# Attention heads in pairs on opposite partition halves, in a two-block transformer kernel on one core

## The chip, the core and the metric

The kernel runs on one core of a Trainium2 chip. The metric is the time on the device in microseconds; 2528.64 us is the median of three runs before (2525.15 to 2530.93). The core has a matrix engine (TensorE, PE in the profile, with its weight loads as PEld), VectorE (DVE), ScalarE (ACT), GpSimd (POOL), a queue engine (SyncE, SP) that issues the transfers, and 16 DMA engines. Matrix products write to PSUM, which DVE and ACT read.

## What is computed

Two transformer blocks on 256 tokens of width 2048, in float32. The change lies in the first block's mixer, which has four kinds of heads. Cut to what matters:

```python
def fox_attention(q, k, v, f_logit, f_bias):      # 7 heads of 64: "forgetting"
    cum = jnp.cumsum(log_sigmoid(f_logit + f_bias), axis=1)
    s = einsum(q, k) * scale + cum_q - cum_k       # causal
    return einsum(softmax(s), v)

def nsa_attention(...):                            # 8 heads of 64, 2 groups of keys
    o_c = einsum(softmax(q @ kc + bias), vc)       # 15 compressed keys
    o_s = einsum(softmax(q @ k_slc + bias), v_slc) # selected blocks
    o_w = einsum(softmax(q @ k_win + bias), v_win) # window
    return g0 * o_c + g1 * o_s + g2 * o_w

def dilated_attention(q, k, v):                    # 9 heads of 64: 3 dilations x 3
    # per dilation a softmax over its own keys; then a softmax over the three
    # log-sums of heads i, 3 + i, 6 + i weighs their outputs
    ...

def diff_attention(q, k, v, lam_vecs, ...):        # 4 heads, two maps of 64 each
    return rms_norm(einsum(softmax(s0) - lam * softmax(s1), v))

o = concat([o_fox, o_nsa, o_dil, o_diff]) @ w_out
```

At 256 tokens all selected blocks and the whole window are kept, so every map is a causal 256 x 256 table with a bias (for the dilated heads with holes). The rest of the network (modulation vectors from `ada_w`, a gated feed-forward layer, a second block with banded, recurrent and memory attention) is the same before and after.

## The kernel before

Every dense product streams its weights from memory in pieces of 128 x 1024 (`piece`, lines 284 to 295): SP loads a piece, ACT rounds it to a high part `Wh` (line 292), DVE takes the rest `Wl` (line 293), and PE multiplies both with activations that are split in the same way (`unit_b`, `unit_a`). Three buffers each hold `W`, `Wh` and `Wl`. After each piece the build calls `trickle`, which may emit one piece of background work, the scaling of a 128 x 1024 block of `ada_w` on DVE (line 431, tile `b`; 192 of them in the kernel), and `step`, which advances the attention heads. `RATES` says how many background pieces go with each weight piece in the five parts of the mixer; `settle` makes sure that enough of them are done before their results are used. So the number of weight pieces and of background pieces is fixed, whatever the heads do.

A head is a Python generator: each `yield` hands the turn back until the next weight piece. `later(n, fn)` starts one n pieces from now; `AT` holds the spacing (forgetting heads 4 pieces apart, selected-block heads 5, dilated triples 4, differential heads 4). The tile framework then orders the instructions of each engine by their order in the program and by its own estimate of when they can run. Loads through `load` (line 195: tables, background pieces) are pinned to program order on SP.

All the heads go through the same helpers:

- `scores` (line 572) makes one map: the upper 128 queries against 256 keys and the lower 128 against 128 keys, two PE products of 64 rows, for forgetting heads each followed by a product of 7 rows that adds the running sums (`sel7`, `ncum`). Each float32 product is two instructions in the trace. DVE adds a table and takes the maximum (line 589), ACT takes the exponential (line 593).
- `weigh` (line 599) scales the map, `pt` transposes it (line 192 on PE, copied by ACT in line 608), `pv` multiplies with the values, 128 rows and 64 columns for these heads: again two products.
- `put` (line 620) splits a head's 64 rows into half of one of the 16 tiles `O`, by line 626 (ACT) and line 627 (DVE).

`fox_head`, `nsa_head` and `dil_triple` handle one forgetting head, one selected-block head (a selected and a window map, then their value products and that of the compressed keys in one sum) and three dilated heads in a row. The queries and keys of head h lie on partitions 0 to 63 or 64 to 127 (`half`), alternating with h for forgetting and dilated heads; for the selected-block heads by group, heads 0 to 3 low and 4 to 7 high. Each score map takes one of four side banks of PSUM (`ps`), and so does each transposed map and each value product; the dense products have four other banks (`pd`). Everything of a head is emitted on its own, so on PE consecutive small products mostly read the same half. `diff_head` is the exception: its two maps, in the low and in the high half, are emitted one behind the other. In the second block, `rw_scan` already alternates its recurrent products between the halves.

`SLOTS`, `BUFS` and `WB` set the buffers: 14 of the 256-column temporaries `q`, 8 maps `e`, 3 transposed maps `pt`, 3 tables `tab`.

Of the kernel before, what the change touches and what calls it, by code (L numbers as in the profile page):

```python
# [111 lines left out]
AT = {"fox": 4, "nsa": 5, "dil": 4, "diff": 4, "pre": 4, "solve": 20, "a": 5, "c": 2}  # L112
# [16 lines left out]
NARROW = {"start"}  # L129

# [16 lines left out]
class Build:  # L147
# [424 lines left out]
    def scores(self, q, k, tab, fox=None):  # L572


        nc = self.nc
        p = self.ps()
        last = fox is None
        self.mm(p[:, 0:256], q[:, 128:256], k, True, last)
        if not last:
            self.mm(p[:, 0:256], fox[0], fox[1], False, True)  # L580
        self.mm(p[:, 256:384], q[:, 0:128], k[:, 0:128], True, last)
        if not last:
            self.mm(p[:, 256:384], fox[0], fox[1][:, 0:128], False, True)
        e = self.tmp((128, 384), tag="e")
        m = self.tiny(2)
        nm = self.tiny(2)
        sm = self.tiny(2)
        for a, (lo, hi, t0) in enumerate(((0, 256, 0), (256, 384, 128))):
            nc.vector.tensor_tensor_reduce(e[:, lo:hi], p[:, lo:hi], tab[:, t0:256], scale=1.0, scalar=-3e38,
                                           op0=OP.add, op1=OP.max, accum_out=m[:, a:a + 1])  # L590
        nc.vector.tensor_scalar(nm, m, -1.0, None, op0=OP.mult)  # L591
        for a, (lo, hi) in enumerate(((0, 256), (256, 384))):
            nc.scalar.activation(e[:, lo:hi], e[:, lo:hi], AF.Exp, bias=nm[:, a:a + 1],  # L593
                                 accum_out=sm[:, a:a + 1])
        return e, m, sm
# [24 lines left out]
    def put(self, n, ps):  # L620

        t, h = n // 2, (n % 2) * 64
        if self.O[t] is None:
            self.O[t] = self.slot(dt=F32R)
        o = self.O[t][h:h + 64]
        self.nc.scalar.copy(o[:, :256], ps)
        self.nc.vector.tensor_tensor(o[:, 256:], ps, o[:, :256], op=OP.subtract)
# [6 lines left out]
    def fox_head(self, h):  # L634
        q, k = self.hq[h], self.hk[h]
        tab = self.table(0)
        yield from self.wait(lambda: self.ncum is not None)
        e, m, sm = self.scores(q, k, tab, (self.sel7[h], self.ncum))
        self.weigh(e, self.recip(sm))
        yield  # L640
        t = self.pt(e)
        yield
        hf = (h % 2) * 64
        p = self.ps()[hf:hf + 64, :256]
        self.pv(p, self.fv[0][:, 64 * h:64 * h + 64], self.fv[1][:, 64 * h:64 * h + 64], t)
        self.put(h, p)

    def fox_cum(self):
# [28 lines left out]
        yield  # L677
        p = self.ps()
        self.mm(p[:7, 0:128], a[:, 0:7], self.C["trif"])
        self.mm(p[:7, 128:256], a[:, 0:7], self.ones, True, False)  # L680
        self.mm(p[:7, 128:256], a[:, 7:14], self.C["trif"], False, True)
        t = self.slot()
        v.tensor_copy(t[:7, :256], p[:7, :256])
        self.ncum = t[:7, :256]
# [100 lines left out]
    def nsa_head(self, h):  # L785
        nc = self.nc
        g = h // 4
        hf = 64 * g
        q = self.nq[h % 4][hf:hf + 64]
        n = 7 + h  # L790
        tab = self.table(1 + h)
        es = []
        yield
        for br, k in ((1, self.nks), (2, self.nkw)):
            e, m, sm = self.scores(q, k[hf:hf + 64], tab)
            f = self.recip(sm)
            for a in range(2):
                nc.vector.tensor_tensor(f[:, a:a + 1], f[:, a:a + 1], self.gate[:, 1 - a, h, br:br + 1], op=OP.mult)  # L798
            self.weigh(e, f)
            es.append(e)  # L800
            yield
        ts = [self.pt(e) for e in es]
        yield from self.wait(lambda: self.pct is not None)
        yield
        of = (n % 2) * 64
        p = self.ps()[of:of + 64, :256]
        self.mm(p, self.vcb[:, h, :], self.pct, True, False)
        for b in range(2):
            c = b * 128 + g * 64
            self.pv(p, self.nv[0][:, c:c + 64], self.nv[1][:, c:c + 64], ts[b], False, b == 1)  # L810
        self.put(n, p)

    def dil_triple(self, i):
        nc, v = self.nc, self.nc.vector
        M = self.tiny(6)
        Z = self.tiny(6)
        es = []
        for g in range(3):
            h = 3 * g + i
            tab = self.table(9 + h)  # L820
            yield
            e, m, sm = self.scores(self.dq[h], self.dk[h], tab)
            v.tensor_copy(M[:, 2 * g:2 * g + 2], m)
            v.tensor_copy(Z[:, 2 * g:2 * g + 2], sm)
            es.append(e)
        mx = self.tiny(2)
        v.tensor_tensor(mx, M[:, 0:2], M[:, 2:4], op=OP.max)
        v.tensor_tensor(mx, mx, M[:, 4:6], op=OP.max)
        M3 = M.rearrange("p (g a) -> p g a", g=3)
        v.tensor_tensor(M3, M3, mx[:, None, :].to_broadcast([128, 3, 2]), op=OP.subtract)  # L830
        nc.scalar.activation(M, M, AF.Exp)
        v.tensor_tensor(Z, Z, M, op=OP.mult)
        z = self.tiny(2)
        v.tensor_tensor(z, Z[:, 0:2], Z[:, 2:4], op=OP.add)
        v.tensor_tensor(z, z, Z[:, 4:6], op=OP.add)
        r = self.recip(z)
        v.tensor_tensor(M3, M3, r[:, None, :].to_broadcast([128, 3, 2]), op=OP.mult)
        for g in range(3):
            self.weigh(es[g], M[:, 2 * g:2 * g + 2])
        yield  # L840
        for g in range(3):
            h = 3 * g + i
            n = 15 + h
            t = self.pt(es[g])
            yield
            of = (n % 2) * 64
            p = self.ps()[of:of + 64, :256]
            vv = self.dv[0 if h < 5 else 1]
            c = 64 * (h if h < 5 else h - 5)
            self.pv(p, vv[0][:, c:c + 64], vv[1][:, c:c + 64], t)  # L850
            self.put(n, p)
# [16 lines left out]
    def diff_head(self, h):  # L868
# [4 lines left out]
        for m in range(2):  # L873
            e, _, sm = self.scores(self.fq[h][64 * m:64 * m + 64], self.fk[h][64 * m:64 * m + 64], tab)
            es.append(e)
            fs.append(self.recip(sm))
# [9 lines left out]
        self.pv(p, self.fvv[0][:, 128 * h:128 * h + 128], self.fvv[1][:, 128 * h:128 * h + 128], t)  # L886
# [16 lines left out]
    def mixer(self):  # L903
        self.narrow = "mixer" in NARROW
        I, X = self.I, self.X
        w = "w_in"
        self.consts(1)
        sel = [self.slot(), self.slot()]
        self.load(sel[0][:7, :512], I["const2"][:7, :512])
        self.load(sel[1][:7, :384], I["const2"][:7, 512:])  # L910
# [884 lines left out]
```

## Time and profile before

| | |
|---|---|
| timed runs | 2530.93, 2525.15, 2528.64 us (median 2528.64) |
| the profiled execution | 2534.44 us, its span 2532.7 us |
| TensorE busy, its weight loads | 2440.0 us (96%), 2094.4 us (83%) |
| VectorE busy | 1792.8 us (71%) |
| ScalarE busy | 1292.7 us (51%) |
| DMA, mean over the span | 208 GB/s |

"Busy" counts a product until its modelled end, so two products that follow each other closely overlap in it; what a product takes of the engine is better read from the start of one to the start of the next. The timeline merges like instructions that follow each other into one row: start, length, and how many. A chain of waits is followed back from the last instruction of a stretch: each step is the work that released the next.

### The profile page before, as it was taken

Reading aid. Unit: us, or ns where it says so; the run is one execution under the profiler, and the core shown is the slowest. Engines: PE = TensorE matmul, PEld = TensorE weight load, DVE = VectorE, ACT = ScalarE, POOL = GpSimd, SP = SyncE. Lnnn points to the kernel's source line nnn. Section 1 sums busy time; section 2 is a strip of 40 time slices with the busy share of each in tenths; the row PEclk is TensorE's granted clock in tenths of the full one; section 3 lists DMA queues with packets and bytes.
Section 4 is the critical chain, followed back from the end, with each engine's and each line's share of the span. In section 5 each row is a group of like instructions: output and inputs, shape, how many; then the busy total and the mean of one; then the engine's idle time right before and its main releaser. Section 6 shows DMA issues by size and latency. Waiting matters only on the chain.

```text
span 2532.7 us, 39262 instructions
## 1 busy us (share of the span) xinstructions
PE 2440.0 (96%) x14852; PEld 2094.4 (83%) x14852; DVE 1792.8 (71%) x3379; ACT 1292.7 (51%) x2177; POOL 55.6 (2%) x102
## 2 busy tenths in 40 slices
PE   6889999998799999999999999999999999999999
PEld 5778788776588888888888887888888888888888
DVE  8987767789767765555566788768976766666664
ACT  5345445665544444444455554566554654444443
POOL 0000000000000000000000001000020000000000
PEclk8999999999899999999999999999999999999999
DMA  8998777667578775666656655434453466666675
GB/s 323 342 338 290 223 254 262 213 231 260 191 236 273 265 240 184 193 189 190 187 185 187 210 167 177 144 117 144 157 173 121 136 191 190 190 186 191 189 228 166
DMA packets 161501, 527.51 MB, mean 208 GB/s; under 512 B 22912, under 2 KB 33303, under 8 KB 161184
## 3 DMA queue, kind: packets, MB, share of 16 engines
q1 hardware_dynamic: 157296, 516.35, 62.8%
q0 software_dynamic: 4016, 8.66, 1.0%
q8 instruction: 116, 1.90, 0.3%
q14 instruction: 73, 0.60, 0.1%
HBM read 516.54 MB, written 9.45 MB: 208 GB/s over the span
## 4 chain that ended last, share of the span: by engine, by line
PE 75%; DVE 11%; DMA 8%; issue 3%; ACT 2%; SPq 0%; ACTq 0%; DVEq 0%
PE pd L188 67%; PE ps L188 8%; DVE Wl L293 4%; DMA b<-in_ada_w_dram 4%; DVE b L431 2%; DMA W<-in_w_in_dram 2%; DMA W<-in_w_mem_kv_dram 1%; ACT Wh L292 1%; DMA W<-in_w_out_dram 1%; PE ps L192 1%; DVE dt L223 0%; DVE q L202 0%; DVE q L201 0%; DVE s L208 0%; DVE b L1247 0%
## 5 line engine op out<-in xcount | busy, mean ns | idle before, releaser
L188 PE MATMUL pd<-s,Wh 128*128 128x512 f32 (+1 forms) x5824 | 1447.8, 390 | 40.0 <-ACT Wh L292 20.2
L293 DVE TENSOR_TENSOR Wl<-W,Wh 128x1024 fp32r<-128x1024 f32 x770 | 928.2, 1208 | 536.9 <-ACT Wh L292 517.4
L292 ACT CAST Wh<-W 128x1024 fp32r<-128x1024 f32 x770 | 796.7, 1036 | 961.8 <-PE pd L188 596.9
L188 PEld LDWEIGHTS pd<-s,Wh 128*128 128x128 f32 x5824 | 1030.2, 191 | 228.0 <-ACT Wh L292 25.7
L188 PEld LDWEIGHTS pd<-s,Wl 128*128 128x128 f32 x5584 | 765.5, 191 | 66.7 <-DVE Wl L293 12.8
L188 PE MATMUL pd<-s,Wl 128*128 128x256 f32 x5584 | 791.9, 284 | 8.0 <-DVE Wl L293 7.8
L431 DVE SCALAR_TENSOR_TENSOR b<-b,tq 128x1024 f32<-128x1024 f32 x192 | 233.0, 1220 | 53.3 <-DMA b<-in_ada_w_dram 53.0
L188 PE MATMUL pd<-Wh,s 128*128 128x512 f32 (+4 forms) x576 | 164.4, 363 | 3.6 <-ACT Wh L292 3.5
L188 PEld LDWEIGHTS pd<-Wh,s 128*128 128x128 f32 x576 | 103.9, 190 | 20.9 <-ACT Wh L292 5.9
L223 DVE TENSOR_TENSOR dt<-pd,dt 128x256 f32<-128x256 f32 x289 | 110.6, 418 | 12.1 <-ACT dt L222 11.8
L188 PE MATMUL pd<-Wl,s 128*128 128x512 f32 (+4 forms) x288 | 105.5, 366 | 6.8 <-DVE Wl L293 6.8
L222 ACT COPY dt<-pd 128x256 f32<-128x256 f32 x289 | 94.7, 370 | 21.8 <-PE pd L188 19.9
L188 PE MATMUL ps<-s 64*128 64x256 f32 (+7 forms) x356 | 84.8, 369 | 5.2 <-DVE s L1553 3.0
L188 PEld LDWEIGHTS ps<-s 64*128 64x128 f32 (+4 forms) x356 | 55.0, 187 | 28.1 <-issue 11.6
L188 PEld LDWEIGHTS pd<-Wl,s 128*128 128x128 f32 x288 | 54.6, 189 | 18.2 <-DVE Wl L293 11.1
L593 ACT ACTIVATE e<-e,y 128x256 f32<-128x256 f32 x80 | 35.7, 448 | 27.5 <-DVE y L591 27.4
L188 PE MATMUL ps<-q,con 128*128 128x256 f32 x132 | 39.4, 404 | 10.7 <-ACT q L1032 3.0
L208 DVE TENSOR_TENSOR s<-q,s 128x256 fp32r<-128x256 f32 x104 | 39.8, 422 | 5.8 <-ACT s L207 5.5
L207 ACT CAST s<-q 128x256 fp32r<-128x256 f32 x104 | 37.8, 404 | 9.4 <-DVE q L1083 5.1
L188 PEld LDWEIGHTS ps<-q,con 128*128 128x128 f32 x132 | 22.7, 193 | 19.8 <-ACT q L519 4.5
L188 PE MATMUL ps<-pt,s 128*64 128x128 f32 (+3 forms) x176 | 37.4, 341 | 1.7 <-ACT pt L608 1.7
L599 ACT ACTIVATE e<-e,y 128x256 f32<-128x256 f32 x88 | 34.9, 449 | 7.5 <-DVE y L798 3.8
(292 smaller groups left out, 1339.3 us busy)
## 6 DMA issues: line engine op xcount, KB each, us to landing
W<-in_w_in_dram SPq DMA_DIRECT2D x334, 512.0 KB, 3.8
b<-in_ada_w_dram SPq DMA_DIRECT2D x192, 512.0 KB, 5.4
W<-in_ffn_w_gate_dram SPq DMA_DIRECT2D x88, 512.0 KB, 3.7
W<-in_ffn_w_up_dram SPq DMA_DIRECT2D x88, 512.0 KB, 4.0
W<-in_ffn_w_down_dram SPq DMA_DIRECT2D x80, 512.0 KB, 3.6
W<-in_w_mem_kv_dram SPq DMA_DIRECT2D x32, 512.0 KB, 6.6
W<-in_w_out_dram SPq DMA_DIRECT2D x32, 512.0 KB, 4.6
W<-in_w_o_dram SPq DMA_DIRECT2D x32, 512.0 KB, 3.9
```

Of the source, the lines that this page charges most:

```text
L188: self.nc.tensor.matmul(out, lhsT, rhs, start=start, stop=stop)
L192: self.nc.tensor.transpose(out, in_, self.ident[p0:p0 + n, p0:p0 + n])
L207: self.nc.scalar.copy(out[:, :256], src)
L208: self.nc.vector.tensor_tensor(out[:, 256:], src, out[:, :256], op=OP.subtract)
L222: self.nc.scalar.copy(t, ps[:, 256:512])
L223: self.nc.vector.tensor_tensor(t, ps[:, :256], t, op=OP.add)
L292: nc.scalar.copy(Wh[:, :n], W[:, :n])
L293: nc.vector.tensor_tensor(Wl[:, :n], W[:, :n], Wh[:, :n], op=OP.subtract)
L431: nc.vector.scalar_tensor_tensor(W, W, 1.0, self.crow[half], op0=OP.mult, op1=OP.mult, accum_out=acc[:, k:k + 1])
L593: nc.scalar.activation(e[:, lo:hi], e[:, lo:hi], AF.Exp, bias=nm[:, a:a + 1], accum_out=sm[:, a:a + 1])
L599: self.nc.scalar.activation(e[:, lo:hi], e[:, lo:hi], AF.Copy, scale=f[:, a:a + 1])
```

## The change

Two heads of opposite halves are handled together, and their products are emitted in turn, one of each head. `scores` takes a list of heads and gives each its own PSUM bank; `pv` takes a list too and writes the two heads into the two halves of one bank. Forgetting heads go in the pairs (0, 1), (2, 3), (4, 5) and head 6 alone, 8 pieces apart; selected-block heads j and j + 4, 10 apart; the dilated heads run as two tasks, the triples 0 and 1 together as the pairs (0, 3), (1, 4), (6, 7), and triple 2 as (2, 5) and 8 alone. The running sums and the selector rows stand in both halves (partitions 0 to 6 and 64 to 70). `put` writes a whole tile for a pair, which moves heads to other places in `O`; the rows of `w_out` are permuted on the way to device memory to match (`HEADS`, `ROWS`). `q` goes from 14 to 12 buffers, `pt` from 3 to 4. The calls of `pv` and `scores` in `diff_head` and `a_head` take the new form and emit what they emitted before, but for the order: the differential head's two maps now alternate.

```diff
-BUFS = {"q": 14, "dt": 6, "e": 8, "pt": 3, "tab": 3, "b2": 3, "tq": 1}
+BUFS = {"q": 12, "dt": 6, "e": 8, "pt": 4, "tab": 3, "b2": 3, "tq": 1}
-AT = {"fox": 4, "nsa": 5, "dil": 4, "diff": 4, ...}
+AT = {"fox": 8, "nsa": 10, "dil": 8, "diff": 4, ...}
+HEADS = (0, 1, 2, 3, 4, 5, 7, 11, 8, 12, 9, 13, 10, 14, 15, 18, 16, 19, 17, 20, 21, 22, 6, 23)
+ROWS = {"w_out": np.concatenate([np.arange(64 * h, 64 * h + 64) for h in HEADS] + [np.arange(1536, 2048)])}

-    def scores(self, q, k, tab, fox=None):
...
+    def scores(self, heads):
+        ps = [self.ps() for _ in heads]
+        for lo, hi, q0 in ((0, 256, 128), (256, 384, 0)):
+            n = hi - lo
+            for p, (q, k, _, fox) in zip(ps, heads):
+                self.mm(p[:, lo:hi], q[:, q0:q0 + 128], k[:, 0:n], True, fox is None)
+            for p, (_, _, _, fox) in zip(ps, heads):
+                if fox is not None:
+                    self.mm(p[:, lo:hi], fox[0], fox[1][:, 0:n], False, True)
+        out = []
+        for p, (_, _, tab, _) in zip(ps, heads):
+            e = self.tmp((128, 384), tag="e")
...
+            out.append((e, m, sm))
+        return out

-    def pv(self, o, v0, v1, t, start=True, stop=True):
-        self.mm(o, v0, t[:, 0:256], start, False)
-        self.mm(o[:, 128:256], v1, t[:, 256:384], False, stop)
+    def pv(self, heads, start=True, stop=True):
+        for o, v0, v1, t in heads:
+            self.mm(o, v0, t[:, 0:256], start, False)
+        for o, v0, v1, t in heads:
+            self.mm(o[:, 128:256], v1, t[:, 256:384], False, stop)
+
+    def halves(self, p, heads):
+        return [p[64 * a:64 * a + 64, :256] for a in range(len(heads))]

-    def put(self, n, ps):
-        t, h = n // 2, (n % 2) * 64
+    def put(self, t, ps, rows=slice(0, 128)):
...
+        o = self.O[t][rows]
+        self.nc.scalar.copy(o[:, :256], ps[rows, :256])
+        self.nc.vector.tensor_tensor(o[:, 256:], ps[rows, :256], o[:, :256], op=OP.subtract)

+    def fox_heads(self, hs):
+        tab = self.table(0)
+        yield from self.wait(lambda: self.ncum is not None)
+        es = []
+        for e, m, sm in self.scores([(self.hq[h], self.hk[h], tab, (self.sel7[h], self.ncum[h % 2])) for h in hs]):
+            self.weigh(e, self.recip(sm))
+            es.append(e)
+        yield
+        ts = [self.pt(e) for e in es]
+        yield
+        p = self.ps()
+        self.pv([(o, fv(0, h), fv(1, h), t) for o, h, t in zip(self.halves(p, hs), hs, ts)])
...
     def fox_cum(self):
...
+        both = [slice(0, 7), slice(64, 71)]
+        for s in both:
+            self.mm(p[s, 0:128], a[:, 0:7], self.C["trif"])
+            self.mm(p[s, 128:256], a[:, 0:7], self.ones, True, False)
+            self.mm(p[s, 128:256], a[:, 7:14], self.C["trif"], False, True)
+        for s in both:
+            v.tensor_copy(t[s, :256], p[s, :256])

+    def nsa_heads(self, j):
+        hs = (j, j + 4)
+        tabs = [self.table(1 + h) for h in hs]
...
+        for br, k in ((1, self.nks), (2, self.nkw)):
+            maps = self.scores([(self.nq[j][s], k[s], tab, None) for s, tab in zip(rows, tabs)])
...
+            yield
+        ts = [[self.pt(e) for e in pair] for pair in es]
...
+        for o, h in zip(os, hs):
+            self.mm(o, self.vcb[:, h, :], self.pct, True, False)
+        for b in range(2):
+            self.pv([(os[g], vv(0, g), vv(1, g), ts[b][g]) for g in range(2)], False, b == 1)
+        self.put(3 + j, p)

+    def dil_triples(self, run, pairs):
...
+        for hs, _ in pairs:
+            tabs = [self.table(9 + h) for h in hs]
+            yield
+            maps = self.scores([(self.dq[h], self.dk[h], tab, None) for h, tab in zip(hs, tabs)])
...
+        yield
+        for hs, tile in pairs:
+            ts = [self.pt(es[h]) for h in hs]
+            yield
+            p = self.ps()
+            if len(hs) == 2:
+                self.pv([(o, vv(0, h), vv(1, h), t) for o, h, t in zip(self.halves(p, hs), hs, ts)])
+                self.put(tile, p)
...
     def mixer(self):
...
+        for a in (0, 64):
+            self.load(sel[0][a:a + 7, :512], I["const2"][:7, :512])
+            self.load(sel[1][a:a + 7, :384], I["const2"][:7, 512:])
```

## Rows read from the trace of the kernel before

**Rows 1.** The page, part 1: busy us (share of the span), instructions.

```profile
PE 2440.0 (96%) x14852; PEld 2094.4 (83%) x14852; DVE 1792.8 (71%) x3379; ACT 1292.7 (51%) x2177; POOL 55.6 (2%) x102
```

**Rows 2.** Busy time by stretch: engines in us, then clock, DMA share, GB/s.

```profile
263.00:385.00 122.00, 121.64 (x711) 98.13 (x710) 86.92 (x223) 58.41 (x133) 0.00 (x0) 0.96 0.70 237
385.00:545.00 160.00, 157.23 (x877) 126.81 (x875) 115.70 (x341) 95.74 (x235) 0.00 (x0) 1.00 0.69 235
545.00:681.00 136.00, 107.25 (x540) 86.44 (x539) 123.24 (x271) 80.76 (x162) 0.00 (x0) 0.90 0.71 232
1400.00:2000.00 600.00, 589.60 (x4367) 500.91 (x4366) 465.21 (x1028) 331.71 (x562) 44.72 (x78) 1.00 0.49 154
```

**Rows 3.** The chain of waits from 263 to 385 us: shares by line.

```profile
by line: PE pd L188 64.4%; PE ps L188 29.2%; PE ps L192 3.7%; DVE b L431 0.9%; DVE Wl L293 0.9%; DVE q L742 0.2%; issue 0.1%; DVE y L727 0.1%; DVE q L740 0.1%; DVE y L435 0.1%; DVE y L729 0.1%; DVE y L730 0.1%; DVE mod L419 0.1%; DVE y L738
```

**Rows 4.** The chain of waits from 385 to 545 us: shares by line.

```profile
by line: PE pd L188 33.3%; PE ps L188 18.5%; DMA b<-in_ada_w_dram 12.6%; issue 5.2%; DVE b L431 4.8%; PE ps L192 4.7%; DVE Wl L293 4.2%; DMA W<-in_w_in_dram 3.2%; ACT e L593 2.8%; ACT e L599 1.8%; ACT Wh L292 1.3%; SPq L195 1.2%; DVE e L589
```

**Rows 5.** PE around one forgetting head in time: start us, duration us, instructions.

```profile
305.08 0.29 PE L188 MATMUL pd<-Wl,s 128*128 128x280 f32 x1
305.21 0.29 PE L188 MATMUL pd<-Wh,s 128*128 128x280 f32 x1
305.43 2.15 PE L188 MATMUL ps<-s 64*128 64x256 f32 x8
307.51 0.73 PE L188 MATMUL pd<-s,Wh 128*128 128x512 f32 x2
```

**Rows 6.** PE, value product of one forgetting head.

```profile
302.12 0.86 PE L188 MATMUL ps<-pt,s 128*64 128x256 f32 x4
302.91 0.40 PE L188 MATMUL pd<-Wh,s 128*128 128x280 f32 x1
```

**Rows 7.** PE, scores of one selected-block map.

```profile
373.64 0.92 PE L188 MATMUL ps<-s 64*128 64x256 f32 x4
374.49 0.73 PE L188 MATMUL pd<-s,Wh 128*128 128x512 f32 x2
```

**Rows 8.** PE, value products of one selected-block head.

```profile
384.61 0.65 PE L188 MATMUL ps<-s 128*64 128x256 f32 x2
...
386.49 0.41 PE L188 MATMUL pd<-Wh,s 128*128 128x320 f32 x1
```

**Rows 9.** PE, two dilated maps side by side, first place.

```profile
487.74 0.93 PE L188 MATMUL ps<-s 64*128 64x256 f32 x8
488.60 0.86 PE L188 MATMUL ps<-pt,s 128*64 128x256 f32 x4
```

**Rows 10.** PE, two dilated maps side by side, second place.

```profile
491.09 1.57 PE L188 MATMUL ps<-s 64*128 64x256 f32 x8
492.59 0.65 PE L188 MATMUL ps<-pt,s 128*64 128x256 f32 x2
```

**Rows 11.** PE, the two maps of one differential head.

```profile
547.29 0.93 PE L188 MATMUL ps<-s 64*128 64x256 f32 x8
548.15 0.74 PE L188 MATMUL pd<-s,Wl 128*128 128x256 f32 x4
```

**Rows 12.** PE, recurrent products with alternating output halves.

```profile
1665.47 0.69 PE L188 MATMUL ps<-e,s 128*64 128x64 f32 x16
1665.99 0.64 PE L188 MATMUL ps<-s,e 128*64 128x64 f32 x16
```

**Rows 13.** Both instructions of put: duration ns min/median/max, first and last start.

```profile
L626 ACT CAST s<-ps x24: 350/366/370, 271.6 to 529.9; 64x256 fp32r<-64x256 f32 x24
...
L627 DVE TENSOR_TENSOR s<-ps,s x24: 407/422/429, 272.0 to 531.5; 64x256 fp32r<-64x256 f32 x24
```

**Rows 14.** DVE, 262 to 545 us, the score reduces: busy, mean ns | idle.

```profile
L589 DVE CUSTOM_DVE_ANT_0 e<-ps,tab 128x256 f32<-128x256 f32 x68 | 22.0, 351 | 15.3 <-PE ps L188 15.1
```

**Rows 15.** PE groups by shape: the forgetting heads' running sums.

```profile
L188 PE MATMUL ps<-s,y 128*7 128x128 f32 x4 | 0.8, 274 | 0.0
```

**Rows 16.** DMA issues: the mask tables; KB each, median us to landing.

```profile
tab<-in_tabs_dram SPq DMA_DIRECT2D x28, 128.0 KB, 3.7
```

More of the change, by code (lines that the diff above doesn't have):

```diff
@@ L794, in nsa_head @@
         for br, k in ((1, self.nks), (2, self.nkw)):
[L795 to L800, printed above, removed]
+            maps = self.scores([(self.nq[j][s], k[s], tab, None) for s, tab in zip(rows, tabs)])
+            for h, (e, m, sm) in zip(hs, maps):
+                f = self.recip(sm)
+                for a in range(2):
+                    nc.vector.tensor_tensor(f[:, a:a + 1], f[:, a:a + 1], self.gate[:, 1 - a, h, br:br + 1], op=OP.mult)
+                self.weigh(e, f)
@@ L808, in nsa_head @@
         for b in range(2):
[L809 to L813, printed above, removed]
+            vv = lambda t, g: self.nv[t][:, b * 128 + g * 64:b * 128 + g * 64 + 64]
+            self.pv([(os[g], vv(0, g), vv(1, g), ts[b][g]) for g in range(2)], False, b == 1)
+        self.put(3 + j, p)
+    def dil_triples(self, run, pairs):
         nc, v = self.nc, self.nc.vector
[L815 to L820, printed above, removed]
-            yield
[L822 to L839, printed above, removed]
@@ new lines, in dil_triples @@
+        M = {i: self.tiny(6) for i in run}
+        Z = {i: self.tiny(6) for i in run}
+        es = {}
+        for hs, _ in pairs:
+            tabs = [self.table(9 + h) for h in hs]
+            yield
+            maps = self.scores([(self.dq[h], self.dk[h], tab, None) for h, tab in zip(hs, tabs)])
+            for h, (e, m, sm) in zip(hs, maps):
+                g, i = divmod(h, 3)
+                v.tensor_copy(M[i][:, 2 * g:2 * g + 2], m)
+                v.tensor_copy(Z[i][:, 2 * g:2 * g + 2], sm)
+                es[h] = e
@@ L872, in diff_head @@
         yield
-        for m in range(2):
-            e, _, sm = self.scores(self.fq[h][64 * m:64 * m + 64], self.fk[h][64 * m:64 * m + 64], tab)
+        rows = (slice(0, 64), slice(64, 128))
+        for e, _, sm in self.scores([(self.fq[h][s], self.fk[h][s], tab, None) for s in rows]):
             es.append(e)
@@ L954, in mixer @@
         self.begin(self.fox_cum)
-        for h in range(7):
-            self.later(AT["fox"] * h, lambda h=h: self.fox_head(h))
+        for i, hs in enumerate(((0, 1), (2, 3), (4, 5), (6,))):
+            self.later(AT["fox"] * i, lambda hs=hs: self.fox_heads(hs))
         self.rate = RATES[1]
@@ L970, in mixer @@
         self.begin(self.nsa_compress)
-        for h in range(8):
-            self.later(8 + AT["nsa"] * h, lambda h=h: self.nsa_head(h))
+        for j in range(4):
+            self.later(8 + AT["nsa"] * j, lambda j=j: self.nsa_heads(j))
         self.rate = RATES[2]
@@ L983, in mixer @@
         self.unit_a(X, w, [(DIL_V + 320, 256)], 256, keep(self.dv[1], 256))
-        for i in range(3):
-            self.later(4 + AT["dil"] * i, lambda i=i: self.dil_triple(i))
+        for i, (run, pairs) in enumerate((((0, 1), (((0, 3), 7), ((1, 4), 8), ((6, 7), 10))),
+                                          ((2,), (((2, 5), 9), ((8,), 11))))):
+            self.later(4 + AT["dil"] * i, lambda run=run, pairs=pairs: self.dil_triples(run, pairs))
         self.rate = RATES[3]
@@ L1757, in lay_features, with lay_blocks @@
     return x[0].T.reshape(8, 2, 128, 256).transpose(0, 2, 1, 3).reshape(8, 128, 512)
-def lay_blocks(w, specs):
+def lay_blocks(w, specs, rows=None):
     w = w.reshape(-1, w.shape[-1])
+    if rows is not None:
+        w = w[rows]
     out = []
```

112 lines of the change are left out of this document (47 added, 65 removed).

## The prediction

> **What bounds the kernel now.** The order of reading was: the shares of the engines, the same by stretch of time, the chain of waits in the stretches that the change touches, and then TensorE's own order in time around single heads. The shares say that TensorE is busy 96% of the span, DVE 71%, ACT 51% [rows 1]. By stretch that is not one kernel but three [rows 2]. From 263 to 385 us (forgetting heads, the compressed keys, the first selected-block heads) PE works 121.64 of 122 us. From 385 to 545 us (the other selected-block heads, the dilated heads) it works 157.23 of 160 us, but DVE 115.70 and the DMA engines 69% beside it. From 545 to 681 us (differential heads, output projection, the rest of the background scaling of ada_w) DVE works 123.24 of 136 us and PE only 107.25: there the supply of weights is the bound, with a fixed number of pieces. The chain tells the same more sharply. Before 385 us, 64.4 + 29.2 + 3.7 = 97% of it is PE [rows 3]: a microsecond taken off PE is a microsecond. From 385 to 545 us PE has 33.3 + 18.5 + 4.7 = 56.5%; the rest are ada_w transfers, DVE splitting weights, and issue [rows 4]: PE just keeps up with its weights, and both are late in turns.
>
> **What a small burst costs today.** The change alters the order of small PE products, so the unit is a burst of them between dense products, from its first start to the next dense start. Forgetting head: eight instructions, 305.43 to 307.51 = 2.08 us; and the dense product ahead of it held the slot 0.22 us (305.21 to 305.43) where its like took 0.13 (305.08 to 305.21), so 0.09 us to get in: 2.17 us [rows 5]. I take the same 0.09 for each burst. Its value product: 302.12 to 302.91, 0.79 + 0.09 = 0.88 us [rows 6]. One selected-block map: 0.85 + 0.09 = 0.94 us [rows 7]. The value products of such a head (compressed, selected and window part, ten instructions): 1.88 + 0.09 = 1.97 us [rows 8].
>
> **What a pair will cost.** The trace has the operation already, by chance. A differential head's two maps read partitions 0 to 63 and 64 to 127, and the eight instructions of both take 547.29 to 548.15 = 0.86 us [rows 11], against 0.85 us for the four of one map. Two dilated maps side by side take 0.86 us in one place [rows 9] and 1.50 in another [rows 10]; heads alternate between the halves, and the two places are what opposite and equal halves would give. So a pair in opposite halves costs one burst. For the value products (128 rows, 64 columns, outputs in the two halves of one bank) the nearest rows are the recurrent products: 16 instructions of 64 columns with alternating output halves, 1665.47 to 1665.99 = 0.52 us, 0.065 us for two [rows 12]; the 256-column instructions of a single head run one after the other [rows 6]. I take a pair as one burst here too. Bounds: one burst (this row) and two bursts (no overlap for long moving operands).
>
> Of that the Trainium skill speaks against the value products: "TensorE: Matmul & The Clock Gate", Part 3, The mechanism, says that a weight load overlaps running products only when the row group differs, and both halves of a value pair use all rows. In the recurrent row 0.065 us for two leaves no room for two weight loads one after the other, so this trace contradicts it at 64 columns; by that rule the pairs would gain little.
>
> **The sum on PE.** Forgetting scores: 7 bursts become 4 (three pairs and head 6): 3 x 2.17 = 6.5 us. Their value products: 3 x 0.88 = 2.6. Selected-block scores: 16 become 8: 8 x 0.94 = 7.5. Value products: 8 become 4: 4 x 1.97 = 7.9. Dilated scores: 9 maps become four pairs and one single, 5 x 0.94 = 4.70; today five single ones (the kind of rows 7), the overlapped two (0.95) and the serial two (1.59) make 7.24: 2.5. Dilated value products: 9 become 5: 4 x 0.88 = 3.5. Differential: overlapped today in three of the four heads [rows 11], 0. Together 30.5 us. Against it: the running sums are made twice, six more products at 0.2 us at most (0.8 us for four [rows 15]), I take 0.7 in all. And bursts that already stand next to another pay no 0.09: about ten, 1.0 us. Net 28.8 us of PE time: 11.8 before 385 us (all of the forgetting heads, 4 of 16 maps and 2 of 8 value products of the selected-block heads, less 0.7 and half of the 1.0), 17.0 after it.
>
> **The other edits.** `put` runs 13 times instead of 24, at the same length: 11 x 0.366 = 4.0 us less on ACT and 11 x 0.422 = 4.6 us less on DVE [rows 13]; neither ends before 385 us, after it this is a small part of the relief there. Reduces, exponentials and weighings keep their number (68 reduces [rows 14]) but come two heads at a time; before 385 us DVE's 86.92 and ACT's 58.41 of 122 us hide that, and if that cover went, the price is the second head's two reduces, 2 x 0.351 us a pair. Tables: four loads for the forgetting heads instead of seven, but now two in a step with three buffers. In the dilated run the second table of pairs two and three waits for a reduce of the pair before, on SP, with weight loads queued behind it: 0 to 2 x 3.7 us [rows 16]; I take 0, since SP runs pieces ahead, and leave it to the share below. Two more loads of the selector rows stand ahead of the first dense stretch, covered by PE work: 0. The permuted rows of w_out change where data lies, not how much. The temporaries `q` fall from 14 to 12, `pt` rises from 3 to 4: of 1400 to 2000 us PE is idle 10.4 [rows 2], mostly in the recurrent heads, which use `q` most. Bounds -1 (a transposed map that comes free earlier) to +10 (that idle time twice over); I take 0, as 98% busy PE is the nearest row.
>
> **What arrives at the end.** Before 385 us PE is the chain: 11.8 count in full. After it bounds are 0 (supply alone sets the pace) and 17.0; I take PE's share of the chain, 56.5%: 9.6. What follows from 545 us on has a fixed number of pieces and starts earlier by the same. 11.8 + 9.6 = 21.4 us. The profiled execution took 2534.44 us (span 2532.7 and 1.7 around it): 2513.0. The median of the timed runs, 2528.64, is 5.8 below it; the same gain gives 2507.2, and I forecast 2507.
>
> **Rivals.**
> Supply takes the second stretch: once PE is quicker, the ada_w transfers and DVE set the pace from 385 us on. For it: 43% of that chain, and 545 to 681 us, where the same supply is the bound at 232 GB/s, no more than the 235 here [rows 2]. Against it: DVE there has 91% to do, here 72%. Only 11.8 us arrive: 2516.8.
> The value pairs don't overlap: 2.6 + 7.9 + 3.5 = 14.0 of the 28.8 go, and the gain shrinks to 21.4 x 14.8 / 28.8 = 11.0: 2517.6. Against it rows 12. The rule of the Trainium skill named above would do the same.
> The `q` buffers cost their 10 us: 2507 + 10 = 2517.
> Slower: PSUM. The side work has four banks; a pair takes two for its scores, four transposes take four. PE runs in order, so a product that waits for a bank holds the dense ones behind it, until DVE has done the four reduces of a pair, 4 x 0.351 = 1.4 us [rows 14]. 17 score steps and 13 groups of transposes at 1.4 us are 42.0 us, less 28.8: +13.2, 2542. It decides from these 30 waits costing 0.96 us each. For it: reduces already wait for PE, not PE for them, 15.3 us [rows 14], so today no bank is short; that speaks against it.
> It doesn't do what it says: pairs run serially and nothing moves, 2528.6. Rows 11 all but exclude it.
>
> **How the numbers follow.** Forecast 60%, in its own range 2499 (all 28.8) to 2514; supply 22%; value pairs 3%; `q` 5%; PSUM 8%; no overlap 2%. A change under 0.2%, 5.1 us, can't be told from none. The forecast, 18 of the 22, 3 and 4 of the 5 are faster: 85%. The rest of those (5) and the last (2) fall within it: 7%; PSUM 8% slower. The range 2497 to 2522 holds the forecast nearly whole and the supply, value and `q` cases as far as they are faster, about 82%.
>
> **What would show it.** In the changed kernel: a selected-block score burst of eight instructions in 0.86 us, a forgetting pair of sixteen in 2.1, a value pair of eight in 0.79, twenty in 1.9. The last two-map burst of the differential heads comes about 21 us earlier. PE's share of the chain after 385 us falls and the share of ada_w transfers and DVE rises; if it rises to 545-us levels, the supply rival was right. The stretch of the recurrent heads keeps its length, or `q` was the cost. PE waiting for a reduce ahead of scores or transposes would be the PSUM case. The prediction is wrong if bursts halve and the end doesn't move, or if they don't halve.

## The result, and the profile after

The changed kernel took 2491.65 us (median of four runs, 2488.18 to 2494.37) beside 2526.91 us for the kernel before on the same chip: ratio 0.9858, 95% interval 0.9838 to 0.9877, 35 us less. On a second chip it took 2493.57 beside 2522.89 us, ratio 0.9887, interval 0.9871 to 0.9903, 29 us less. The forecast was 2507, a gain of 21.4, in a range that ended at 2497: right sign, gain too small by 8 to 14 us. Below, one of the six executions of `e_dil` took 6040.12 us; its median counts it, its ratio does not.

The profiled execution of before (2534.44 us) was longer than any of its timed runs, that of after (2488.18) was the shortest of its first four. So 46 us lie between these two traces, but not all are the change's. Two further traces help: a second one of after (2495.55 us), and one of the kernel before with only the new buffer numbers (`e_bufs` below, 2519.39 us), which differs from after in the pairs and what goes with them (the whole-tile `put`, the second copy of the running sums, the order of the rows of `w_out`).

The page's first part, which answers to [rows 1]:

```profile
PE 2404.4 (97%) x14858; PEld 2074.2 (83%) x14858; DVE 1787.0 (72%) x3369; ACT 1287.9 (52%) x2166; POOL 55.7 (2%) x102
```

PE gave up 35.6 us of busy time, DVE 5.8. The steps on PE look as foretold. Timeline of PE in after: start us, length us, instructions.

```profile
295.51 2.17 PE L193 MATMUL ps<-s 64*128 64x256 f32 x16
297.62 1.67 PE L193 MATMUL pd<-s,Wh 128*128 128x512 f32 x6
...
374.54 0.92 PE L193 MATMUL ps<-s 64*128 64x256 f32 x8
375.39 0.42 PE L193 MATMUL pd<-Wh,s 128*128 128x320 f32 x1
...
389.34 0.65 PE L193 MATMUL ps<-s 128*64 128x256 f32 x4
389.82 1.55 PE L193 MATMUL ps<-pt,s 128*64 128x256 f32 x16
391.30 0.39 PE L193 MATMUL pd<-Wl,s 128*128 128x256 f32 x1
...
446.06 0.87 PE L193 MATMUL ps<-pt,s 128*64 128x256 f32 x8
446.87 0.87 PE L197 MATMUL ps<-con,e 128*128 128x128 f32 x6
```

From start to start: a forgetting pair 2.11 us (single head 2.08, [rows 5]), a selected-block pair 0.85 (single map 0.85, [rows 7]), twenty instructions of value products 1.96 (ten in 1.88, [rows 8]), a value pair 0.81 (single 0.79, [rows 6]). Every pair costs what one head cost, value pairs too; the rule of the Trainium skill that the prediction quoted against them ("TensorE: Matmul & The Clock Gate", Part 3, The mechanism) does not hold here.

Where the time went is best seen by stretches cut at the same work. I cut at the 1200th, 1680th, 2240th and 2640th dense product: forgetting and first selected-block heads; other selected-block and dilated heads; differential heads and output projection. Busy time by stretch of before, then of `e_bufs`, after, and the second trace of after (columns as in [rows 2], the second number is the length):

```profile
260.80:388.60 127.80, 127.44 (x745) 102.68 (x744) 91.65 (x232) 60.01 (x135) 0.00 (x0) 0.96 0.70 236
388.60:537.30 148.70, 146.01 (x814) 117.80 (x813) 104.97 (x314) 88.65 (x217) 0.00 (x0) 1.00 0.68 229
537.30:637.80 100.50, 89.20 (x463) 71.85 (x461) 93.72 (x214) 62.60 (x126) 0.00 (x0) 0.95 0.80 266
```

```profile
257.00:384.60 127.60, 127.25 (x746) 103.06 (x745) 91.94 (x233) 60.12 (x135) 0.00 (x0) 0.96 0.71 240
384.60:531.40 146.80, 145.54 (x813) 117.75 (x813) 105.04 (x315) 88.97 (x217) 0.00 (x0) 1.00 0.68 231
531.40:629.60 98.20, 87.43 (x463) 70.50 (x461) 93.50 (x213) 62.80 (x126) 0.00 (x0) 0.97 0.78 273
```

```profile
253.00:371.00 118.00, 114.07 (x752) 94.59 (x752) 92.19 (x237) 58.64 (x131) 0.00 (x0) 0.99 0.79 265
371.00:501.00 130.00, 128.83 (x810) 107.55 (x809) 104.26 (x310) 85.93 (x211) 0.00 (x0) 1.00 0.80 272
501.00:596.00 95.00, 87.05 (x466) 71.18 (x465) 90.38 (x210) 62.11 (x126) 0.00 (x0) 0.96 0.79 261
```

```profile
256.00:377.00 121.00, 116.57 (x747) 96.21 (x747) 91.72 (x235) 58.94 (x131) 0.00 (x0) 0.96 0.77 256
377.00:510.00 133.00, 129.26 (x814) 108.02 (x813) 104.98 (x311) 86.28 (x211) 0.00 (x0) 1.00 0.78 267
510.00:605.00 95.00, 86.80 (x467) 71.29 (x465) 90.69 (x209) 62.38 (x126) 0.00 (x0) 0.96 0.79 261
```

Taken exactly from start to start of those products, and with the rest of the span (us):

| | until the first cut | first stretch | second | third | after it |
|---|---|---|---|---|---|
| before | 260.8 | 127.9 | 148.6 | 100.5 | 1894.9 |
| `e_bufs` | 257.0 | 127.6 | 146.8 | 98.2 | 1888.0 |
| after, two traces | 253.3, 255.8 | 117.9, 121.6 | 130.3, 132.8 | 94.7, 94.4 | 1890.0, 1889.0 |
| after less `e_bufs` | -3.7, -1.2 | -9.7, -6.0 | -16.5, -14.0 | -3.5, -3.8 | +2.0, +1.0 |
| forecast | 0 | -11.8 | -9.6 | 0 | 0 |

After the last cut before took 5 to 7 us more than the three other traces, `e_bufs` included: scatter of that execution. Against `e_bufs` the pairs are worth 24 to 31 us; the buffers add some 2 by the ratio of the timed runs, 5 at most by its interval. Before the first cut executions scatter as much as the table shows: `x_before` below, the same program as `e_bufs` up to there, took 260.6 us. In the first stretch the two traces of after differ by 3.7 us, and most of that is TensorE's clock (0.99 and 0.96). Length times granted clock, an estimate of the length at full clock where PE is nearly always busy, is 122.7 and 122.5 us in before and `e_bufs`, 116.8 and 116.2 in the two of after: some 6 us for the pairs. In the second stretch the clock was 1.00 throughout.

The chain of waits by line in after, first stretch (253 to 371 us), then second (371 to 501 us):

```profile
by line: PE pd L193 48.4%; PE ps L193 17.2%; DVE b L436 6.2%; DVE Wl L298 5.2%; DMA b<-in_ada_w_dram 4.7%; DMA W<-in_w_in_dram 3.7%; PE ps L197 3.0%; issue 2.8%; ACT Wh L297 2.6%; DVE e L598 2.1%; ACT e L609 1.9%; ACT e L602 1.7%; ACT s L97
...
by line: PE pd L193 58.1%; PE ps L193 8.7%; PE ps L197 5.4%; issue 3.6%; DVE Wl L298 3.6%; DMA b<-in_ada_w_dram 3.5%; DMA tab<-in_tabs_dram 3.1%; DVE b L436 3.0%; DVE e L598 2.4%; ACT e L602 2.1%; ACT Wh L297 1.6%; ACT e L609 1.2%; DVE s L6
```

PE's share fell from 97% [rows 3] to 68.6% in the first, and rose from 56.5% [rows 4] to 72.2% in the second, where the prediction looked for a fall. The recurrent heads, which use `q` most, did not change: 589.83 us of PE in 600 (1350 to 1950 us), as before [rows 2].

### The profile page after: what moved, and what is told of

The parts are those of the page before. It is cut to its first block, busy times and chain, and to the rows that moved or that the text cites. A ratio compares the mean times of both kernels' runs of the same rounds, so it can differ in the third digit from the quotient of the medians.

```text
span 2486.3 us, 39252 instructions
## 1 busy us (share of the span) xinstructions
PE 2404.4 (97%) x14858; PEld 2074.2 (83%) x14858; DVE 1787.0 (72%) x3369; ACT 1287.9 (52%) x2166; POOL 55.7 (2%) x102
## 4 chain that ended last, share of the span: by engine, by line
PE 78%; DVE 12%; DMA 5%; ACT 2%; issue 2%; POOL 0%; SPq 0%; DVEq 0%; ACTq 0%
PE pd L193 70%; PE ps L193 7%; DVE Wl L298 4%; DVE b L436 2%; DMA W<-in_w_in_dram 2%; DMA b<-in_ada_w_dram 1%; DMA W<-in_w_mem_kv_dram 1%; ACT Wh L297 1%; PE ps L197 1%; DMA W<-in_w_out_dram 1%; DVE e L598 0%; DVE dt L228 0%; DVE b L1279 0%; DVE q L207 0%; DVE q L206 0%
## 5 line engine op out<-in xcount | busy, mean ns | idle before, releaser
L436 DVE SCALAR_TENSOR_TENSOR b<-b,tq 128x1024 f32<-128x1024 f32 x192 | 232.8, 1218 | 10.3 <-DMA b<-in_ada_w_dram 9.9
L193 PE MATMUL ps<-s 64*128 64x256 f32 (+7 forms) x356 | 65.8, 366 | 4.5 <-DVE s L1585 3.6
L193 PEld LDWEIGHTS ps<-s 64*128 64x128 f32 (+4 forms) x356 | 44.0, 186 | 21.2 <-issue 6.1
L193 PE MATMUL ps<-q,con 128*128 128x256 f32 x132 | 38.8, 400 | 12.9 <-ACT q L1064 3.7
```

The costliest lines, as they stand in the source:

```text
L193: self.nc.tensor.matmul(out, lhsT, rhs, start=start, stop=stop)
L436: nc.vector.scalar_tensor_tensor(W, W, 1.0, self.crow[half], op0=OP.mult, op1=OP.mult, accum_out=acc[:, k:k + 1])
```

## Experiments

Theory A: in the second stretch PE alone sets the pace, so all of its saving arrives there; the chain's DMA and DVE steps have no time to give. Theory B, the prediction's: PE and supply are late in turns, and a share arrives. Beside these: how much is the overlap and how much the mere grouping, and what the whole-tile `put` is worth. A ratio is to the kernel before on the same chip.

**Buffers alone** (`e_bufs`, the kernel before):

```diff
-BUFS = {"q": 14, ..., "pt": 3, ...}
+BUFS = {"q": 12, ..., "pt": 4, ...}
```

> The kernel before with the buffers of the change alone: 12 temporaries q instead of 14, 4 transposed maps pt instead of 3; every product and its order in the program as before. Theory A (the gain is PE time, and all of it arrives, since PE sets the pace in both stretches; my 56% for the second stretch was the wrong step): 0 to -6 us, all of it ahead of the heads or in small stalls, so about 2523 against 2527. Theory B (PE gave only the 21 us that I forecast and other edits gave the rest): -10 us or more, 2517 or less.

2520.93 us, ratio 0.9992 (0.9981 to 1.0004). No cost; a gain of 2 us by the ratio, between a loss of 1 and a gain of 5 by its interval.

**Grouping without overlap** (`e_same`): pairs of heads in the same half, (0, 2), (1, 3) and so on, `put` by single heads:

```diff
-        for j in range(4):
-            self.later(8 + AT["nsa"] * j, lambda j=j: self.nsa_heads(j))
+        for j, hs in enumerate(((0, 2), (1, 3), (4, 6), (5, 7))):
+            self.later(8 + AT["nsa"] * j, lambda hs=hs: self.nsa_heads(hs))
```

> Everything of the change but the opposite halves: heads go two at a time in the same spacing and with the same buffers, but the two of a pair read the same partition half and write the same output half, so their products can't overlap; forgetting pairs (0, 2), (1, 3), (4, 6), selected-block pairs (0, 2), (1, 3), (4, 6), (5, 7), dilated pairs (0, 4), (1, 3), (5, 8). Each head is put on its own, w_out is not permuted. Theory A: two selected-block maps take about 1.5 us in a burst instead of 0.86, and the time is that of the buffers alone within 5 us, about 2522. Theory B: grouping by itself gives the rest, 2515 or less.

2512.66 us, ratio 0.9952 (0.9940 to 0.9965): 12 us less, 10 without the buffers' 2. PE of `e_same` in time, a forgetting pair and a selected-block pair:

```profile
275.82 3.46 PE L193 MATMUL ps<-s 64*128 64x256 f32 x16
279.21 3.25 PE L193 MATMUL pd<-s,Wh 128*128 128x512 f32 x8
...
385.32 1.57 PE L193 MATMUL ps<-s 64*128 64x256 f32 x8
386.82 0.41 PE L193 MATMUL pd<-Wh,s 128*128 128x320 f32 x1
```

Sixteen instructions of one half take 3.39 us where two single heads took 2 x 2.08; eight take 1.50, two single maps 2 x 0.85. So the second head in a row saves 0.77 and 0.20 us besides the 0.09 of getting in. Grouping alone gives 12 of the 29 to 35 us. The other 17 to 23 us came with the opposite halves; the whole-tile `put`, which `e_same` leaves out and which is priced below at some 7 us, is among them.

**Parts alone**: `e_fox`, `e_nsa`, `e_dil` pair one kind of heads, `e_foxnsa` two, all with the new buffers and the single-head code for the others (here the forgetting heads, as in `e_nsa` and `e_dil`):

```diff
-        for i, hs in enumerate(((0, 1), (2, 3), (4, 5), (6,))):
-            self.later(AT["fox"] * i, lambda hs=hs: self.fox_heads(hs))
+        for h in range(7):
+            self.later(AT["fox"] * h, lambda h=h: self.fox_head(h))
```

> Of the pairs only those of the forgetting heads (with the 12 and 4 buffers); selected-block and dilated heads one at a time as before. Theory A (PE time arrives in full, each part by itself): 9.1 - 0.7 us of PE and about 2 us of the buffers, -10 us, 2515 against 2525. Theory B (the parts only pay together, because fewer small products in one stretch let the weights of the next run ahead): -4 us or less.

> Only the selected-block heads in pairs (with the buffers). Theory A: 15.4 us of PE and 2 of the buffers, -17 us, 2508. Theory B: -9 us or less.

> Only the dilated heads in pairs (with the buffers). Theory A: 6.0 us of PE and 2 of the buffers, -8 us, 2517. If the three parts less twice the buffers come to the -33 of the whole, nothing is lost or gained between them. Theory B: within 3 us of the kernel before.

> Pairs for the forgetting and the selected-block heads, dilated heads single. Forgetting pairs alone were worth 2.5 us, selected-block pairs alone 17.8, both with the new buffers (2 us). If the parts add, 18 us less than before, 2505. If the forgetting pairs pay only when the heads behind them on PE are short too (they end in the stretch where the selected-block heads begin), 18 plus the 7 to 9 us that the sum of the parts lacks against the whole: 25 to 27 less, 2496 to 2498.

Forgetting pairs alone: 2521.29, ratio 0.9990 (0.9978 to 1.0001). Selected-block: 2504.96, 0.9933 (0.9921 to 0.9945). Dilated: 2512.02, 0.9958 (0.9945 to 0.9971). The first two together: 2498.51, 0.9898 (0.9884 to 0.9913), the 25 us of the second guess. The forgetting pairs, which should have paid 10 us, paid almost nothing alone and 7 to 9 on top of the others. Their products did shrink: 64-row and 7-row products take 15.8 us of the first stretch in `e_fox`, 22.0 in `e_bufs`. But PE waited 4.1 us there, against 0.3, and 14.0 us in the third stretch, against 10.8. Why less of that wait is left when the selected-block heads are pairs too, these runs don't settle.

In the second stretch, against `e_bufs`, each of these runs got shorter by what PE's small products saved there (from start to start): 11.8 us for 11.5 in `e_nsa`, 6.9 for 6.2 in `e_dil`, 10.3 for 10.7 in `e_foxnsa`, and nothing for 0.6 in `e_fox`. The second stretch of `e_nsa`:

```profile
382.50:517.50 135.00, 133.39 (x813) 109.62 (x812) 105.07 (x313) 88.08 (x214) 0.00 (x0) 1.00 0.76 256
```

That is theory A's count.

**The waits of the first stretch.** PE's waits in after, 253 to 371 us (what it waited for: us in total, times, longest):

```profile
PE ps L197 <- ACT e L609: 2.0, 2, 1.8
PE ps L193 <- DVE y L695: 1.5, 1, 1.5
PE ps L193 <- DVE mod L424: 0.3, 1, 0.3
```

Before had only the last of these. In the first, the transposes of a pair, one step behind its scores, wait until two maps, not one, have been weighed (line 609). In the second the running sums wait for the logarithm ahead of them (line 695). Both wait for work that goes through DVE, where the scaling pieces stand too. `e_noada` leaves out the scaling of `ada_w` while the first stretch runs (33 pieces, those modulation values are constants):

```diff
+        if self.idle:
+            self.pin(nc.vector.memset(acc[:, k:k + 1], 0.5))
+        else:
+            self.load(W, src)
...
```

> The changed kernel without the background scaling of ada_w (transfer and DVE work) while the selected-block and dilated projections run, some 45 pieces of 512 KB; their sums are set to a constant, so those modulation vectors are left out of the result. Theory A: PE sets the pace there, so the stretch keeps its length within 5 us, about 2488 to 2492. Theory B: the transfers and DVE hold a third of that stretch, and without them it gets 10 us shorter or more, 2481 or less.

2482.86 us, ratio 0.9831 (0.9816 to 0.9846), 7 to 14 us below after, between the two forecasts. All 28 pieces of the first stretch are out:

```profile
255.20:366.60 111.40, 110.90 (x751) 92.89 (x750) 61.98 (x204) 58.19 (x131) 0.00 (x0) 1.00 0.48 149
```

It takes 111.5 us with 0.5 of waiting, instead of 117.9 and 121.6 with 3.9 and 4.4; beside 116.8 and 116.2 at full clock that is 5 us. Of the second stretch's 28 only 5 are out, so it says little there.

**PE's time doubled back** (`e_dup`): after, with the scores of the selected-block and dilated pairs made three times:

```diff
-        for lo, hi, q0 in ((0, 256, 128), (256, 384, 0)):
+        for lo, hi, q0 in ((0, 256, 128), (256, 384, 0)) * times:
```

> The changed kernel with the score products of the selected-block and dilated heads emitted three times, with the same result. Each of 13 steps gets 2 x 0.65 us more PE time, 16.9 us in all, nothing else. Theory A: PE sets the pace where they stand, so +15 to +18 us, about 2508 against 2491.7. Theory B: by PE's share of the chain after 385 us about 56% arrives, +9 to +10 us, 2501.

2517.79 us, ratio 0.9974 (0.9960 to 0.9987): 22 to 29 us more than after (from the two ratios of after), above both forecasts, for 16 to 17 us of products, 12.7 of them in the second stretch. That takes 152.7 us, 20 to 22 more. What came on top, PE's waits of `e_dup` from 377 to 530 us:

```profile
PE ps L197 <- ACT e L609: 7.5, 5, 2.5
PE ps L197 <- DVE y L598: 1.5, 1, 1.5
```

Later scores make later maps, and the transposes wait for them. PE's time counts in full here, and these waits come on top.

**More supply in the second stretch** (`e_rates`, after):

```diff
-RATES = (0.5, 0.8, 0.8, 0.8, 1.0)
+RATES = (0.5, 0.7, 1.1, 0.8, 1.0)
```

> The changed kernel with RATES (0.5, 0.7, 1.1, 0.8, 1.0) for (0.5, 0.8, 0.8, 0.8, 1.0): some six pieces of the scaling of ada_w move from the first stretch and from the differential heads into the second stretch (dilated projections). Theory (after the change the second stretch is PE's alone: its length did not move when all these pieces were taken out, 131.0 against 130.3 us, while the first has 3.9 us and the third 8.2 us of PE idle): the second stretch keeps its length, the others lose idle time, 3 to 8 us faster than the changed kernel. Rival (the supply sets the second stretch too): the second gets longer by as much, within 2 us of the changed kernel, or slower.

2504.11 us beside 2493.57 for after on this chip: 10 us slower, where A had been read to promise 3 to 8 faster. The expectation was badly founded: it took `e_noada` for a run without supply in the second stretch, which it wasn't. And three of the eight added pieces fell into the first stretch (31 for 28), five into the second (33 for 28). Busy time of `e_rates` by stretch:

```profile
255.60:382.30 126.70, 120.60 (x750) 99.62 (x750) 94.05 (x240) 57.65 (x130) 0.00 (x0) 0.92 0.73 249
382.30:517.20 134.90, 130.10 (x813) 108.30 (x812) 111.33 (x324) 86.95 (x212) 0.00 (x0) 1.00 0.81 286
517.20:616.10 98.90, 86.17 (x463) 71.90 (x462) 90.80 (x207) 61.06 (x126) 0.00 (x0) 0.93 0.74 250
```

The first stretch is 5 to 9 us longer, the second 2 to 5, the third 4. The first needs no supply to explain it: 126.7 us at a granted clock of 0.92 are 116.6 at full clock, as in after. In the second, at 1.00, PE waited 4.8 us, where it waited 1.2 and 3.7 in after. So the supply is not the bound of the second stretch, but it stands close behind.

**The same 28 pieces out of the second stretch**, after and before (`x_after`, `x_before`; pieces 100 to 127, those modulation values are constants):

```diff
+        if 100 <= self.count < 128:
+            self.pin(nc.vector.memset(acc[:, k:k + 1], 0.5))
+        else:
...
```

> The changed kernel without the 28 pieces of the scaling of ada_w (numbers 100 to 127) that run in the second stretch, 1680th to 2240th dense product; those modulation values are constants instead. DVE has 34 us less there and the DMA engines 14 MB less. Theory (PE alone sets that stretch after the change too): its length stays within 3 us of 130.3 and 132.8 us, the two traces with them. Rival (PE and supply are late in turns, as the chain of waits says): it falls by 5 us or more, to 125 or less, and what PE waits there for weighed maps or weights goes.

> The kernel before with the new buffer numbers, without the same 28 pieces. With them the second stretch takes 146.8 us. Theory (PE alone sets it, the chain's DMA and DVE steps have no time to give): 145 to 148 us. Rival, by the reading of the forecast (43% of that chain is supply): removing it takes 5 us or more off, 142 or less; were the chain's shares time that can be had, up to 0.435 x 147 = 64 us.

After: 2493.27 us, ratio 0.9877 (0.9861 to 0.9894), what after has with these pieces. Before: 2520.03, ratio 0.9988 (0.9979 to 0.9998), what `e_bufs` has with them. The second stretch of `x_before`, then of `x_after`:

```profile
388.50:532.80 144.30, 144.22 (x814) 117.39 (x813) 80.81 (x290) 90.44 (x218) 0.00 (x0) 1.00 0.49 152
```

```profile
379.80:508.00 128.20, 126.97 (x812) 107.54 (x811) 75.63 (x284) 86.25 (x211) 0.00 (x0) 1.00 0.55 171
```

DVE has 24 to 29 us less to do, the DMA share falls from 0.68 to 0.49 and from 0.78 or more to 0.55, and the stretch shortens by 2.5 us before and 2.0 to 4.5 after. B is out: of the 43.5% of the chain that was not PE, some 64 us, 2.5 could be had. The run takes out only the `ada_w` part of it (17.4%, [rows 4]), but no more is left to have: PE works 144.22 of the 144.30 us that remain. A holds before the change. After it 128.3 us lie 2.0 and 4.5 under the two traces, where A had said 3 at most and B 5 at least: PE sets that stretch but for a few us, which may be the supply's.

**`put` in two halves** (`e_put`, `e_put_again`, one kernel on two chips, the second time beside after):

```diff
+        for lo in range(rows.start, rows.stop, 64):
+            r = slice(lo, lo + 64)
+            o = self.O[t][r]
...
```

> The changed kernel with put in two 64-row halves for every pair, 11 x 0.37 us more on ACT and 11 x 0.42 us more on DVE, as before the change. Theory A (DVE and ACT have room there): within 3 us of the changed kernel, 2492. Theory B (the relief on DVE is part of what came over 28.8): +4 us or more, 2496.

> The changed kernel with put in two halves of 64 rows, once more, now beside the changed kernel itself on one chip: 24 instead of 13 calls of put, 11 x 0.366 us more on ACT and 11 x 0.422 us more on DVE, PE's work the same. Theory A (the relief of DVE in the supply-bound stretches is a part of the gain): 5 to 11 us slower than the changed kernel here as well. Rival (the first result was the difference between two chips): within 3 us of it.

> The changed kernel again, on the chip of the next three, with a second trace. The first comparison gave a ratio of 0.9858 (0.9838 to 0.9877), 35 us, from four runs each. If the whole effect is real, 0.985 to 0.988 here, 2491 to 2496 us. Its second trace should have the same lengths of the three stretches of dense products (117.9, 130.3, 94.7 us in the first trace) within 2 us; what differs by more between the two is scatter of one execution and not the change.

After again: 2493.57 us, ratio 0.9887, a little under the effect expected; its first stretch is 3.7 us and its second 2.5 us longer than in the first trace, where 2 were expected, its third the same. With halves 2496.40 us (ratio 0.9903, 0.9890 to 0.9916), then 2502.93 (0.9914, 0.9897 to 0.9930) beside after's 0.9887: 7 us by the ratios, 9 by the medians. The chip was not the reason, though the two intervals of that chip overlap a little and one of the six runs with halves took 2490.61. In both traces the third stretch is longer, 98.8 and 97.6 us for 94.7 and 94.4. PE's waits in it, after:

```profile
PE ps L197 <- DVE e L910: 2.2, 2, 1.5
PE pd L193 <- DVE s L213: 2.2, 1, 2.2
PE pd L193 <- DVE Wl L298: 1.3, 3, 0.6
PE ps L193 <- ACT pt L618: 1.1, 2, 0.6
...
```

and with halves (`e_put_again`):

```profile
PE pd L193 <- DVE Wl L298: 8.1, 8, 2.1
PE pd L193 <- ACT Wh L297: 2.8, 3, 2.1
PE ps L197 <- DVE e L912: 0.4, 1, 0.4
...
```

All calls of `put` lie before this stretch. With 11 more of them its weights are late, 10.9 us of waiting on `Wl` and `Wh` instead of 1.3. The first stretch too has 6.1 us of waiting for 3.9 and 4.4.

That the copies act on the third stretch through DVE's time is not shown. `e_rates`, with whole-tile puts, has the same waits there and takes 98.8 us:

```profile
PE pd L193 <- DVE Wl L298: 8.5, 6, 4.0
PE pd L193 <- ACT Wh L297: 4.2, 1, 4.2
```

And `e_bufs`, with 24 puts, waits only 3.7 us for `Wl` and `Wh` in its 98.2 us. The timed runs show that whole-tile puts are worth some 7 us in this kernel; by which path, they leave open.

## Why the prediction fell short, step by step

**The pairs' cost: right.** Bursts of 0.85, 2.11, 0.81 and 1.96 us against 0.86, 2.1, 0.79 and 1.9. Small products on PE (64-row, 7-row, 64-column, transposes) take, in the first two stretches, 38.8 and 44.1 us in `e_bufs`, 28.9 or 30.6 and 28.6 in after: 24 to 25 us saved, 25 to 27 against the trace of before; the sum said 28.8.

**"After it ... I take PE's share of the chain, 56.5%: 9.6": wrong.** This is the step that failed. 14.0 to 16.5 us arrived, all that PE saved there (44.1 - 28.6 = 15.5). PE worked 98% of that stretch; with so little idle time its saving could not go elsewhere until another engine filled up, and DVE had 30% to spare. The chain walked through transfers and splits that finished just in time; with the scaling pieces taken out, the stretch gave 2.5 us (`x_before`). "Perfetto Trace Analysis", Identifying the Most-Contended Engine, in the Trainium skill says to take the engine with the highest occupancy (TensorE by its weight loads) as the bottleneck and to optimize that first. 126.81 us of weight loads against DVE's 115.70 [rows 2] name PE, and `x_before` agrees.

**"11.8 count in full": too much.** 6.0 to 9.7 us arrived, some 6 in both traces by length times granted clock. The small products gave 8.2 to 9.9 of PE's time, and some 4 us came back as waits for weighed maps and for the running sums. The sentence that reduces and exponentials are hidden by DVE's 86.92 of 122 us, with 2 x 0.351 us a pair if the cover went, had the right mechanism and too small a price: one such wait was 1.8 us.

**Relief by `put`: 4.6 us of DVE not counted.** Whole-tile puts are worth some 7 us by the timed runs, 3 to 4 of them in the third stretch of the traces; the prediction itself had called the third one supply-bound, and let it only start earlier. The path from the copies to that stretch stays open. "TensorEngine Tiling (Array Packing)", PSUM Bottleneck, in the Trainium skill warns that after faster products the copies out of PSUM may become the bottleneck, and advises to make such an access across several tiles of one bank. The 7 us agree with the advice; that the copies bound anything here no run shows.

**Start and buffers.** 1.2 to 3.7 us came before the first cut, no more than the same program scatters there (257.0 in `e_bufs`, 260.6 in `x_before`), and some 2 from the buffers; neither was counted.

**Rivals.** Supply taking the second stretch: refuted (`x_after`). Value pairs, no overlap: refuted by the bursts. `q`: refuted (`e_bufs`, recurrent stretch). PSUM: refuted; in the second stretch of after PE waits 0.5 us for a score reduce (line 598) and 0.4 for a `put` (line 642), 0.9 and 1.1 in the second trace.

```profile
PE ps L197 <- DVE y L598: 0.5, 1, 0.5
PE ps L193 <- DVE s L642: 0.4, 1, 0.4
```

The range's lower end, 2497, lay 2 us under "all 28.8" and left out every gain that is not PE's.

## What to carry to other kernels

Where an engine is busy 98% of a stretch, count its saving there in full up to the next engine's busy time; a chain of waits in which other engines alternate with it shows what is just in time, not what is short. To know it, take the suspected supply out of one stretch and see whether it shortens. And price what a grouping does to the other engines' instruction counts: eleven fewer copies, 4.6 us of DVE, came with some 7 us here. Before two executions are compared by stretch, compare their granted clocks.

## What the runs showed of the hardware

Two heads of the same half cost less side by side than apart: 3.39 us for 16 instructions against 2 x 2.08, so in one long burst the second head's products cost 0.8 us less than alone (0.2 us less for maps of four instructions). In `e_dup` 24 instructions of opposite halves in a row took 2.17 us, eight 0.85: 0.66 us for each further eight.

```profile
380.63 2.23 PE L193 MATMUL ps<-s 64*128 64x256 f32 x24
382.80 0.42 PE L193 MATMUL pd<-Wh,s 128*128 128x320 f32 x1
```

Time and granted clock mostly go together from run to run, but not always. Of the twelve runs of `e_fox` the shortest, 2511.32 us, had a mean granted clock of 0.992, the longest, 2525.66, 0.985; the four runs of `e_after`, 2489.47 to 2499.93, all had 0.987. The clock has two levels here, 1.2 and 2.4 GHz (0.50 and 1.00), and means between them are a mixture. What the lower one costs, PE of before shows: the eight instructions of a forgetting head take 2.08 us at 1.00 [rows 5] and 3.71 from start to start at 0.50 (the last line is busy time in that stretch, columns as in [rows 2]).

```profile
328.90 3.79 PE L188 MATMUL ps<-s 64*128 64x256 f32 x8
332.61 3.48 PE L188 MATMUL pd<-s,Wh 128*128 128x512 f32 x8
...
328.90:332.30 3.40, 3.40 (x9) 1.87 (x9) 3.21 (x6) 0.23 (x1) 0.00 (x0) 0.50 0.23 47
```

In the first stretch the mean was 0.92 in `e_rates`, where PE was idle 6.1 us, and 1.00 in `e_noada`, where it was idle 0.5; but `e_bufs`, with 0.3 us idle, had 0.96, so idle time in the stretch isn't all of it, and what else lowers it these runs don't show. `x_after`, the same program as after up to the second stretch, took 123.8 us in the first, at 0.93: 115.1 by length times clock, beside 116.8 and 116.2.
